# A hybrid encoder block on one core: new DRAM layouts in the mixer, attention scores over 128 partitions, and a different order of products, loads and stores

## The chip, the cores and the metric

The kernel runs on one core of one Trainium2 chip. The metric is the device time of one execution in microseconds (us); lower is better. All engines of the core work at once and meet through semaphores: TensorE (PE) multiplies, VectorE (DVE), ScalarE (ACT) and GpSimd (POOL) compute elementwise, and SyncE (SP) issues most of the transfers. ACT and POOL issue some as well.

## The reference

One layer for 1024 tokens of width 1024, all in float32:

```
h = h + 1/2 * SwiGLU(RMSNorm(h))
u = RMSNorm(h);  z = u @ W_in          # q | k | v | ssm input | gate_attn | gate_ssm
A = neighbourhood_attention(q, k, v)   # 8 heads of 64; 16 x 64 grid of tokens, window 8 x 16
B = s5_branch(ssm input)               # 32 groups of 16 channels, 64 complex states each,
                                       # forward and backward scan, + D*u, gelu, GLU (512 x 512)
h = h + (sig(gate_attn) * (A @ W_a) + sig(gate_ssm) * (B @ W_s)) @ W_out
h = h + 1/2 * SwiGLU(RMSNorm(h))
h = h + (p @ W_ple) * sig(RMSNorm(h) @ W_g);  out = RMSNorm(h)
```

## The kernel before, in words

Every large product is made of float32r matmuls. An operand is split into a high and a low part (ACT casts the high part, DVE subtracts for the low one), and three matmuls of 128x512 take high-high, high-low and low-high (`mm3`, L188; lines L190 to L192 in the profile). Large products are further folded into seven block products (Strassen-Winograd): of one pair of output blocks the seven run in the order of `A7`, into the PSUM accumulators `ACC7 = "ZXYXYXX"`. The sixth product (index 5) leaves the sum that becomes block 22 in X, DVE adds it out of X (`s_evac`, L1535), and the seventh product goes on accumulating in the same X.

The change lies in the **mixer**, the stage between the two feed-forward networks. The main code of the mixer emits these products on PE:

- `proj` (accumulator `sin`): 8 products of 24 matmuls, the input of the state-space branch. Their results go to the DRAM tile `u_d`.
- `value` (accumulator `v`): 8 products of 24 matmuls for v, each for 128 tokens; the results go to `v_d` as high and low part.
- `items`: 12 pairs times 7 block products of 12 matmuls (`px`, `py`, `pz`) for q, k and the gates; the weight blocks `blk` are loaded `LL` products ahead. Results go to `q_d`, `k_d` and `g_d`.

Beside it runs a generator, `mixer_side` (L1315). It holds everything else of the mixer, and the main code calls `tick()` after each step of three matmuls; a `yield n` in the generator lets n steps pass. So the numbers in the yields set how the side work is mixed into the in-order queue of PE: the norm of the second token half (`u_second`), the injections into the states (`inject`, 16 pairs of groups, accumulator `inj`), the attention (64 units of head, row half and column block: `attn_scores` into `s`, `attn_turn` into `pt` two units later, `attn_values` into `O` four units later), the recurrence on POOL (`scan_steps`), the read-out of the states (`ssm_out`, 16 pairs, accumulator `yo`), and the GLU (`glu_load`, `glu_half`, accumulator `glu`). Ahead of block product 78 of 84 stands `drain()`: whatever is left of the generator is emitted there in one piece, with no main product in between.

DVE, ACT, POOL and SP get their order from a scheduler at build time; PE keeps the order of the program. Each queue runs in order. A transfer that SP or ACT issues takes one of eight completion counters in turn (`DMAHW0` to `DMAHW7` in the rows further down) and waits for the last transfer on that counter.

## Time and profile before

| what | value |
|---|---|
| runs before | 2194.84 us median of 2 (2192.94 to 2196.74) |
| the profiled execution's own time | 2193.82 us |
| its span, first to last instruction | 2192.0 us |
| granted TensorE clock, mean over the span | 0.982 |
| PE busy | 2089.9 us, 95% of the span |
| DVE, ACT, POOL busy | 1465.8, 1015.1, 436.4 us |
| moved by transfers | 317.67 MB, 145 GB/s on average |

Times in the views are microseconds from the start of the span, durations of single instructions are nanoseconds where a view says so. A wait is idle time of an engine, put down to what ended it. Matmuls are pipelined: the time from one start to the next is what a matmul costs, not the duration of its row.

### The profile page before, as it was taken

Reading aid. Unit: us, or ns where it says so; the run is one execution under the profiler, and the core shown is the slowest. Engines: PE = TensorE matmul, PEld = TensorE weight load, DVE = VectorE, ACT = ScalarE, POOL = GpSimd, SP = SyncE. Lnnn points to the kernel's source line nnn. Section 1 sums busy time; section 2 is a strip of 40 time slices with the busy share of each in tenths; the row PEclk is TensorE's granted clock in tenths of the full one; section 3 lists DMA queues with packets and bytes.
Section 4 is the critical chain, followed back from the end, with each engine's and each line's share of the span. In section 5 each row is a group of like instructions: output and inputs, shape, how many; then the busy total and the mean of one; then the engine's idle time right before and its main releaser. Section 6 shows DMA issues by size and latency. Waiting matters only on the chain.

```text
span 2192.0 us, 28396 instructions
## 1 busy us (share of the span) xinstructions
PE 2089.9 (95%) x9518; PEld 1684.9 (77%) x9518; DVE 1465.8 (67%) x2470; ACT 1015.1 (46%) x1870; POOL 436.4 (20%) x652
## 2 busy tenths in 40 slices
PE   8999999999999798999993799999999999999998
PEld 3788888888887686777772588878888888888887
DVE  7897866767867545665550467897656655795855
ACT  6443333344454334666553464554333333545543
POOL 0046555530001328886000002000000000000000
PEclk9999999999999899999997899999999999999999
DMA  3434444496334475666555685324232337443302
GB/s 127 149 113 155 129 129 135 133 311 189 107 115 129 121 191 176 188 183 181 162 158 181 211 266 150 81 91 154 82 124 88 115 97 278 137 142 96 116 29 77
DMA packets 239859, 317.67 MB, mean 145 GB/s; under 512 B 55264, under 2 KB 113248, under 8 KB 239712
## 3 DMA queue, kind: packets, MB, share of 16 engines
q1 hardware_dynamic: 200592, 277.02, 40.6%
q10 hardware_dynamic: 36816, 34.63, 4.8%
q0 software_dynamic: 2304, 4.20, 1.1%
q8 instruction: 75, 1.23, 0.2%
q14 instruction: 72, 0.59, 0.1%
HBM read 221.92 MB, written 93.85 MB: 144 GB/s over the span
## 4 chain that ended last, share of the span: by engine, by line
PE 85%; DVE 6%; DMA 3%; SPq 2%; ACT 2%; issue 1%; POOL 0%; ACTq 0%; DVEq 0%
PE dx L190 4%; PE dx L191 4%; PE dx L192 4%; PE gx L190 3%; PE ux L190 3%; PE gx L192 3%; PE ux L192 3%; PE ux L191 3%; PE gx L191 3%; PE dy L191 2%; PE dy L192 2%; PE dy L190 2%; PE px L190 2%; PE px L191 2%; PE px L192 2%; PE gy L190 2%
## 5 line engine op out<-in xcount | busy, mean ns | idle before, releaser
L159 ACT CAST wh<-hbuf 128x512 fp32r<-128x512 f32 x280 | 173.0, 622 | 392.4 <-PE gx L191 84.1
L160 DVE TENSOR_TENSOR wl<-hbuf,wh 128x512 fp32r<-128x512 f32 x280 | 209.9, 752 | 123.6 <-ACT wh L159 121.2
L159 ACT CAST wh<-wblk 128x512 fp32r<-128x512 f32 x190 | 118.0, 622 | 191.2 <-PE dx L191 82.5
L190 PE MATMUL dx<-ah,wh 128*128 128x512 f32 x416 | 163.5, 393 | 0.4 <-DVE hbuf L694 0.3
L160 DVE TENSOR_TENSOR wl<-wblk,wh 128x512 fp32r<-128x512 f32 x190 | 130.5, 689 | 49.0 <-ACT wh L159 41.4
L192 PE MATMUL dx<-ah,wl 128*128 128x512 f32 x416 | 161.9, 389 | 0.0
L191 PE MATMUL dx<-al,wh 128*128 128x512 f32 x416 | 161.9, 389 | 0.0
L160 DVE TENSOR_TENSOR al<-araw,ah 128x512 fp32r<-128x512 f32 x154 | 106.1, 693 | 51.8 <-PE dx L191 21.2
L190 PE MATMUL gx<-xh,wh 128*128 128x512 f32 x320 | 124.9, 390 | 1.2 <-DVE c L581 1.2
L190 PE MATMUL ux<-xh,wh 128*128 128x512 f32 x320 | 125.0, 391 | 0.0
L192 PE MATMUL gx<-xh,wl 128*128 128x512 f32 x320 | 124.5, 389 | 0.0
L192 PE MATMUL ux<-xh,wl 128*128 128x512 f32 x320 | 124.5, 389 | 0.0
L191 PE MATMUL ux<-xl,wh 128*128 128x512 f32 x320 | 124.5, 389 | 0.0
L191 PE MATMUL gx<-xl,wh 128*128 128x512 f32 x320 | 124.5, 389 | 0.0
L159 ACT CAST ah<-araw 128x512 fp32r<-128x512 f32 x154 | 94.9, 619 | 47.1 <-PE dx L191 14.2
L1155 POOL TENSOR_TENSOR sc<-X,rho 128x128 f32<-128x128 f32 x128 | 77.7, 607 | 82.0 <-ACT X L1138 72.0
L190 PEld LDWEIGHTS dx<-ah,wh 128*128 128x128 f32 x416 | 78.1, 188 | 18.6 <-DVE hbuf L694 1.2
L428 DVE TENSOR_TENSOR hbuf<-hbuf 128x512 f32<-128x512 f32 x120 | 90.4, 754 | 2.7 <-DMA hbuf<-in_wu 0.6
L191 PEld LDWEIGHTS dx<-al,wh 128*128 128x128 f32 x416 | 78.1, 188 | 16.8 <-issue 0.7
L192 PEld LDWEIGHTS dx<-ah,wl 128*128 128x128 f32 x416 | 78.1, 188 | 16.3
L190 PE MATMUL px<-xh,wh 128*128 128x512 f32 x192 | 78.8, 410 | 12.1 <-DVE z L1535 11.2
L421 POOL DMA_DIRECT2D wblk<-in_wout x16 | 14.1, 934 | 339.5 <-ACT wblk L420 339.2
(396 smaller groups left out, 5785.7 us busy)
## 6 DMA issues: line engine op xcount, KB each, us to landing
araw<-a_d SPq DMA_DIRECT2D x154, 256.0 KB
a_d<-c SPq DMA_DIRECT2D x148, 256.0 KB
wblk<-in_wd SPq DMA_DIRECT2D x88, 256.0 KB
hbuf<-in_wg SPq DMA_DIRECT2D x40, 512.0 KB
hbuf<-in_wu SPq DMA_DIRECT2D x40, 512.0 KB
blk<-in_win SPq DMA_DIRECT2D x48, 256.0 KB
hbuf<-in_xT SPq DMA_DIRECT2D x32, 256.0 KB
h_d<-hbuf ACTq DMA_DIRECT2D x32, 256.0 KB
```

The lines of the kernel that those rows point to most:

```text
L159: A.copy(hi, src)
L160: return eng.tensor_tensor(lo, src, hi.bitcast(F32), ALU.subtract)
L190: T.matmul(o, lhsT=wh, rhs=xh, start=first, stop=False, skip_group_check=more)
L191: T.matmul(o, lhsT=wh, rhs=xl, start=False, stop=False, skip_group_check=more)
L192: T.matmul(o, lhsT=wl, rhs=xh, start=False, stop=last, skip_group_check=more)
L421: G.dma_start(blk[i], src, accum_op=ALU.add)
L428: V.tensor_tensor(b11, (b12, b22, None, None, b21)[i - 2], b11, ALU.subtract)
L1155: G.tensor_tensor(sc, both, rho4, ALU.mult)
```

## The change

All of it is in the mixer.

1. **Layouts in DRAM.** `u_d` and `y_d` become [4, 128, 8, 128] (channel, phase, chunk) and `v_d` becomes one block per head of 256 rows by 512. A store of `sin` and a load for the GLU are now one transfer of 128 partitions in place of eight of 16, and a load of v one transfer in place of four. The loads `ut` and the stores `ys` become two transfers of 64 KB in place of one of 128 KB.
2. **Scores.** One tile holds the high part of k in partitions 0 to 63 and the low part in 64 to 127; q is held as two tiles, the high part twice and the low part twice. Both matmuls of a score contract over 128 partitions. Before, the second one contracted over 64. The product of the two low parts is now included.
3. **Values.** Four accumulators are open at once and the weights go in the outer loop, so each weight block is loaded when it is near.
4. **Order of the block products.** The first product of a pair runs ahead of the last one of the pair before.
5. **Stores.** Stores of the gates, q and k are collected and issued at the third step of the next product; those of the gates all by SP.
6. **Mixing.** Injections take 2 steps each instead of 3, and all wait for the last `sin` store; an attention unit takes 3 steps instead of 4; the first loads of `ssm_out` go into the last units of the attention, and a pair of it takes 1 or 2 steps. The norm of the second half comes 4 steps earlier and its POOL part follows it, with the store of `s_d` issued by POOL.
7. **Buffers.** The pool `m` has 24 tiles (22), the pool `k4` two (3), and `LL` is 4 (5).

```diff
-    u_d = dtile("u_d", [NPD, P, NCH])
+    u_d = dtile("u_d", [4, P, L, NCH])
-    v_d = dtile("v_d", [SEQ, 1024])
+    v_d = dtile("v_d", [NH, 4 * GRID, 512])
-    y_d = dtile("y_d", [NPD, P, NCH])
+    y_d = dtile("y_d", [4, P, L, NCH])
...
     def u_second():
-        yield 10
+        yield 6
         un[1].stat()
         yield 1
+        for j in (0, 1, 2, 3, 4, 5, 6, 7):
+            u_norm(j, 1)
+            yield 1
+        yield 3
         for k in range(4):
-            u_norm(k, 1)
-            yield 1
-            u_norm(4 + k, 1)
             G.tensor_tensor(h[4 + k][1], h[k][1], h[4 + k][1], ALU.add)
...
     def load_u(pr):
         ut = ta("ut", [P, 2, NCH])
-        nc.sync.dma_start(ut, u_d[2 * pr:2 * pr + 2].rearrange("g p c -> p g c"))
+        for g in range(2):
+            i0 = (2 * pr + g) % 8 * 16
+            nc.sync.dma_start(ut[:, g], u_d[pr // 4, i0:i0 + 16].rearrange("i s c -> s i c"))
...
-            nc.scalar.dma_start(y_d[2 * pr:2 * pr + 2].rearrange("g p c -> p g c"), ys)
+            for g in range(2):
+                o0 = (2 * pr + g) % 8 * 16
+                nc.scalar.dma_start(y_d[pr // 4, o0:o0 + 16].rearrange("o t c -> t o c"), ys[:, g])
...
     def load_v(hd, cb):
-        for g in range(4):
-            nc.sync.dma_start(hl[0:n, g].bitcast(F32),
-                              vdr[4 * g:4 * g + 4, KC0[cb]:KC0[cb] + KNC[cb], hd * 128:(hd + 1) * 128])
+        nc.sync.dma_start(hl[0:n].rearrange("p g d -> p (g d)").bitcast(F32), vdr[hd, :, KC0[cb]:KC0[cb] + KNC[cb]])
...
-        T.matmul(s3, lhsT=q, rhs=kv(khs[hd]), start=True, stop=False)
-        T.matmul(s3, lhsT=q[ds], rhs=kv(kl_["t"])[ds], start=False, stop=True)
+        for a in range(2):
+            T.matmul(s3, lhsT=qs[hd, rb][a][:, ksl(cb)], rhs=kv, start=a == 0, stop=a == 1)
...
     def glu_load(t):
         for m in range(4):
             yt = ygs[t, m] = tmp("yt")
-            yv = yt.rearrange("p (t c) -> p t c", t=4)
-            for g in range(8):
-                nc.sync.dma_start(yv[g * 16:(g + 1) * 16], ydr[8 * m + g][:, 4 * t:4 * t + 4])
+            nc.sync.dma_start(yt, y_d[m, :, 4 * t:4 * t + 4].rearrange("p t c -> p (t c)"))
...
             inject(pr, *ld.pop(pr))
-            yield 3
+            yield 2
...
             scan_steps(2)
-            yield 4
+            if j >= n:
+                lo[j - n] = ssm_load(j - n) if j - n < 3 else None
+            yield 3
         scan_steps(NCH)
...
-            if 0 <= p - 1 < NPAIR:
+            if p > 0:
                 so.pop(p - 1)()
-            yield 2
+            yield 1 + p % 2
...
-            for g in range(8):
-                nc.sync.dma_start(u_d[8 * m + g].rearrange("(s i) c -> i s c", s=L)[:, :, t * 64:(t + 1) * 64],
-                                  su[g * 16:(g + 1) * 16].rearrange("i (s c) -> i s c", s=L))
+            nc.sync.dma_start(u_d[m, :, :, t * 64:(t + 1) * 64],
+                              su.rearrange("i (s c) -> i s c", s=L))
...
+    def values(t):
+        os_ = [bank("v") for _ in range(4)]
         for k in range(NK):
+            load_wv()
...
     items = [(n, i) for n in range(len(pairs)) for i in range(7)]
+    for n in range(7, len(items), 7):
+        items[n - 1:n + 1] = items[n], items[n - 1]
+    later = []
...
-            (nc.scalar if c == "21" else nc.sync).dma_start(g_d[2 * m + second, :, hsl(t)], src)
+            later.append((nc.sync, g_d[2 * m + second, :, hsl(t)], src))
...
             mm3(sacc[a], (hi[:, ksl(k)], lo[:, ksl(k)]), U[A7[i]][k], NEW7[i] and k == 0, k == 3, not NEW7[i])
+            if k == 2:
+                s_store()
+                if i == 1 and n > 0 and pairs[n - 1][0] == "qk":
+                    m = pairs[n - 1][1]
+                    ready.update((2 * m, 2 * m + 1))
             tick()
```

What that does to the queues is seen at three places. The first is PE at the end of a pair of blocks, here the gate pair `px_7784` before and `px_7782` after. Before, the seventh product (weights `wh_7943`) follows the sixth (`wh_7888`) at once:

```order
L190 MATMUL px_7784<-xh_7253,wh_7888 128x512
L191 MATMUL px_7784<-xl_7254,wh_7888 128x512
L192 MATMUL px_7784<-xh_7253,wl_7889 128x512
L190 MATMUL px_7784<-xh_7257,wh_7888 128x512
L191 MATMUL px_7784<-xl_7258,wh_7888 128x512
L192 MATMUL px_7784<-xh_7257,wl_7889 128x512
L190 MATMUL px_7784<-xh_6256,wh_7943 128x512
```

After the change the twelve matmuls of the next pair's first product (`pz_8132`) stand between; the seventh product of the pair (`wh_8036`) comes behind them:

```order
L190 MATMUL pz_8132<-xh_6007,wh_7977 128x512
L191 MATMUL pz_8132<-xl_6008,wh_7977 128x512
L192 MATMUL pz_8132<-xh_6007,wl_7978 128x512
L190 MATMUL px_7782<-xh_6251,wh_8036 128x512
L191 MATMUL px_7782<-xl_6252,wh_8036 128x512
L192 MATMUL px_7782<-xh_6251,wl_8037 128x512
```

So the seventh product has moved behind a product on another accumulator, at eleven of the twelve pairs.

The second place is PE at the first pairs of `ssm_out`. Before, the read-out follows the last main product ahead of the drain (`pz_11079`), pair behind pair:

```order
L190 MATMUL pz_11079<-xh_6007,wh_11017 128x512
L191 MATMUL pz_11079<-xl_6008,wh_11017 128x512
L192 MATMUL pz_11079<-xh_6007,wl_11018 128x512
L1181 MATMUL yo_11144<-ut_11114,emi_11110 128x128
L1183 MATMUL yo_11144<-xs_11128,emi_11110 128x128 x2
L1181 MATMUL yo_11144<-ut_11114,emi_11112 128x128
L1183 MATMUL yo_11144<-xs_11128,emi_11112 128x128 x2
L1181 MATMUL yo_11165<-ut_11120,emi_11116 128x128
L1183 MATMUL yo_11165<-xs_11139,emi_11116 128x128 x2
```

After the change main products (`px_10778`) stand between the pairs:

```order
L1182 MATMUL yo_10794<-ut_10649,emi_10645 128x128
L1184 MATMUL yo_10794<-xs_10752,emi_10645 128x128 x2
L1182 MATMUL yo_10794<-ut_10649,emi_10647 128x128
L1184 MATMUL yo_10794<-xs_10752,emi_10647 128x128 x2
L190 MATMUL px_10778<-xh_5782,wh_10706 128x512
L191 MATMUL px_10778<-xl_5783,wh_10706 128x512
L192 MATMUL px_10778<-xh_5782,wl_10707 128x512
L1182 MATMUL yo_10820<-ut_10679,emi_10675 128x128
L1184 MATMUL yo_10820<-xs_10789,emi_10675 128x128 x2
L1182 MATMUL yo_10820<-ut_10679,emi_10677 128x128
L1184 MATMUL yo_10820<-xs_10789,emi_10677 128x128 x2
```

What moved is the whole end of the generator: 39 main matmuls stand between the last `yo` and the first `glu`, six between each two of the eight GLU steps but the fourth and fifth, where 12 stand, and 87 behind the last GLU matmul, where 72 stood. The first score stands behind 141 main matmuls of the block products, before behind 123.

The third place is SP at the loads for the GLU (`yt`), here with the counters that each row waits for. Before, there are 64 of them, of which the first are:

```order
L1601 DMA hbuf<-h_d 128x512 [waits DMAHW4_49]
L1601 DMA hbuf<-h_d 128x512 [waits DMAHW5_49]
L1283 DMA yt<-y_d 16x4x128 [waits DMAHW7_49]
L1283 DMA yt<-y_d 16x4x128 [waits DMAHW0_49]
L1283 DMA yt<-y_d 16x4x128 [waits DMAHW1_49]
L1283 DMA yt<-y_d 16x4x128 [waits DMAHW2_49]
```

After the change there are eight, in two groups of four, behind seven loads of `hbuf` (the residual stream, 256 KB each):

```order
L1598 DMA hbuf<-h_d 128x512 [waits DMAHW2_49]
L1598 DMA hbuf<-h_d 128x512 [waits DMAHW3_49]
L1274 DMA yt<-y_d 128x512 [waits DMAHW4_49,PE_49]
L1274 DMA yt<-y_d 128x512 [waits DMAHW5_49,PE_49]
L1274 DMA yt<-y_d 128x512 [waits DMAHW6_49,PE_49]
L1274 DMA yt<-y_d 128x512 [waits DMAHW7_49,DMAHW1_49]
L1598 DMA hbuf<-h_d 128x512 [waits DMAHW0_49]
L1533 DMA g_d<-z_11240 128x512 [waits Activation_49]
```

Fifty-six issues are gone from SP there; the tiles that they filled are the same.

More of the change, by code (lines that the diff above doesn't have):

```diff
@@ L1316, in mixer_side @@
         yield from u_second()
[L1317 removed]
+        while 3 not in stored:
             yield 1
[L1319 removed]
+        yield 8
         new_x()
         ld = {}
+        for pr in range(2):
+            ld[pr] = inject_load(pr)
+        yield 6
         for pr in range(NPAIR):
[L1323 to L1330 removed]
+            if pr + 2 < NPAIR:
                 ld[pr + 2] = inject_load(pr + 2)
             inject(pr, *ld.pop(pr))
[L1333 removed]
+            yield 2
         while 0 not in ready:
@@ L1361, in mixer_side @@
                     load_k(hd + 1)
-                if rb == 1 and cb == 2 and hd + 1 < NH and hd + 1 not in khs:
+                if rb == 1 and cb == 2 and hd + 1 < NH and hd + 1 not in khl:
                     load_k(hd + 1)
@@ L1522, in s_out @@
         for i, x in enumerate((hi, lo)):
-            nc.scalar.dma_start((k_d if second else q_d)[m, i, :, hsl(t)], x.bitcast(F32))
+            later.append((nc.scalar, (k_d if second else q_d)[m, i, :, hsl(t)], x.bitcast(F32)))
     def s_evac(n, i):
@@ L1536, in s_evac, with s_store @@
         s_out(n, c, int(c[0]) - 1, int(c[1]) - 1, o[a] if c == "21" else z.pop(c))
+    def s_store():
+        while later:
+            q, dst, src = later.pop(0)
+            q.dma_start(dst, src)
     def s_run(n, i):
@@ L1547, in s_run @@
             s_evac(n, i)
-        if i == 6 and pairs[n][0] == "qk":
-            ready.update((2 * pairs[n][1], 2 * pairs[n][1] + 1))
-    LL, LP = 5, 2
+    LL, LP = 4, 2
     done_ = {"l": 0, "p": 0}
@@ L1560, in s_ahead @@
             done_["p"] += 1
-    for tt in range(NK):
-        if tt == 4:
-            s_ahead(-2)
-        if tt == 6:
-            s_ahead(0)
-        value(tt)
+    for t in range(2):
+        values(t)
     s3s = []
```

117 lines of the change are left out of this document (49 added, 68 removed).

## The prediction

> **What bounds the kernel now.** I read the busy shares first, then the mixer's stages by windows, then what PE waited for, then the rows at the places that the change touches. The page gives PE 95%, which says only that a loss must be looked for in single stages:
>
> ```profile
> PE 2089.9 (95%) x9518; PEld 1684.9 (77%) x9518; DVE 1465.8 (67%) x2470; ACT 1015.1 (46%) x1870; POOL 436.4 (20%) x652
> ```
>
> The mixer runs from 685.0 to 1265.9 us. Cut at the first matmuls of `sin`, `v`, the block products, the scores, `yo`, the idle stretch, `glu` and the last six block products:
>
> ```profile
> core 0: us, PE busy (x) PEld busy (x) DVE busy (x) ACT busy (x) POOL busy (x), PEclk, DMA share, GB/s
> 685.00:740.30 55.30, 48.68 (x203) 38.14 (x202) 44.03 (x47) 25.01 (x39) 26.98 (x16) 0.94 0.42 109
> 740.30:809.20 68.90, 61.08 (x314) 51.07 (x313) 23.06 (x46) 19.46 (x44) 4.13 (x11) 0.93 0.66 172
> 809.20:838.20 29.00, 28.12 (x124) 22.79 (x123) 21.89 (x29) 13.40 (x23) 25.63 (x44) 1.00 0.65 198
> 838.20:1139.50 301.30, 286.51 (x1518) 222.82 (x1518) 181.13 (x420) 176.56 (x389) 161.52 (x331) 0.99 0.59 174
> 1139.50:1176.30 36.80, 26.04 (x193) 23.93 (x191) 10.62 (x34) 19.49 (x49) 0.00 (x0) 0.95 0.84 254
> 1176.30:1209.90 33.60, 0.05 (x1) 0.00 (x0) 0.69 (x1) 7.81 (x12) 0.00 (x0) 0.56 0.35 105
> 1209.90:1244.70 34.80, 28.36 (x96) 21.40 (x97) 13.69 (x21) 13.85 (x23) 0.00 (x0) 0.84 0.56 180
> 1244.70:1265.90 21.20, 18.48 (x74) 14.50 (x72) 14.33 (x21) 11.86 (x19) 0.00 (x0) 0.92 1.03 275
> ```
>
> The sixth stage is the thing to see: 33.6 us without a matmul, every engine nearly idle. Around it the granted clock falls to 0.84 to 0.95. What PE waited for in the mixer:
>
> ```profile
> PE glu L190 <- ACT wgl L159: 39.5, 3, 33.6
> PE px L190 <- DVE z L1535: 11.2, 11, 2.4
> PE yo L1181 <- DMA ut<-u_d: 8.1, 9, 2.1
> PE py L190 <- ACT z L1531: 6.3, 2, 6.0
> PE sin L191 <- DVE xl L160: 5.0, 4, 2.6
> ```
>
> The releaser ACT `wgl` is only the last link: SP's timeline has 64 small issues of 0.48 us each, 30.44 us, and a weight load behind them.
>
> ```profile
> 1175.94 30.44 SPq L1283 DMA_DIRECT2D yt<-y_d  x64
> 833.38 12.38 SPq L1215 DMA_DIRECT2D vhl<-v_d  x16
> ```
>
> The second row is the same fault in the first loads of v. Block weights queue behind them, hence the one wait of 6.0 us above.
>
> **What the work itself costs.** One main matmul, from the first and the thirtieth in a row: (691.60 - 685.02) / 29 = 0.227 us.
>
> ```profile
> 685.02 0.39 PE L190 MATMUL sin<-xh,whh 128*128 128x512 f32 x1
> 691.60 0.39 PE L192 MATMUL sin<-xh,whl 128*128 128x512 f32 x1
> 771.08 1.05 PE L1131 MATMUL inj<-ut,fmi 128*128 128x128 f32 x8
> 771.89 0.48 PE L1439 MATMUL v<-wvh,xh 128*128 128x512 f32 x1
> 772.20 0.40 PE L1440 MATMUL v<-wvl,xh 128*128 128x512 f32 x1
> 1146.14 0.43 PE L1181 MATMUL yo<-ut,emi 128*128 128x128 f32 x2
> 1148.86 0.39 PE L1181 MATMUL yo<-ut,emi 128*128 128x128 f32 x2
> 1046.92 0.34 PE L1234 MATMUL s<-kh,qs 128*128 128x384 f32 x1
> 1047.19 0.44 PE L1235 MATMUL s<-kl,qs 64*128 64x384 f32 x1
> 1047.56 0.53 PE L1251 MATMUL pt<-ident,sm 128*96 128x128 f32 x3
> 1051.19 0.29 PE L1234 MATMUL s<-kh,qs 128*128 128x288 f32 x1
> ```
>
> An injection takes 0.81 us and slows the matmul behind it by 0.08, 0.89 together. Four half pairs of the read-out take 2.72 us, a pair 1.36. A unit of attention with 12 main matmuls takes 1051.19 - 1046.92 = 4.27; less 12 x 0.227, 1.55 are its own. So each stage has this much that is not work:
> - `sin`: 55.3 - 192 x 0.227 - 0.5 for the norm's sum = 11.2
> - `v`: 68.9 - 192 x 0.227 - 16 x 0.89 = 11.1
> - block products ahead of the scores: 29.0 - 123 x 0.227 = 1.1
> - attention: 301.3 - 813 x 0.227 - 64 x 1.55 = 17.5
> - `yo`: 36.8 - 16 x 1.36 = 15.0; the gap: 33.6; `glu`: 34.8 - 96 x 0.227 = 13.0; the last six: 21.2 - 72 x 0.227 = 4.9
>
> Together 107.4 us. PE's queue is in order and no main matmul is added or dropped; the change can take at most these 107 us and whatever a score gets cheaper.
>
> **The change part by part.**
>
> *GLU loads and the end of the generator.* 56 issues of 0.48 us, 27 us, leave SP. Next in line is a chain: store of the last `ys`, load `yt`, gelu, split. Rows of such links:
>
> ```profile
> 1176.79 3.04 DMA y_d<-ys
> 1206.43 2.83 DMA wgs<-in_wglu
> L1287 ACT ACTIVATE yt<-yt x8: 629/629/630, 1183.0 to 1208.0; 128x512 f32<-128x512 f32 x8
> ```
>
> Store 3.0, a load of 256 KB 2.8, one to four gelus 0.6 to 2.5, a split on ACT and DVE some 1.3: 7.7 to 9.6, plus seven loads of the residual on SP ahead of `yt` (at the 275 GB/s of the last window 1.8 MB are 6.7 us, part of which lies beside the store). So 9 to 16 us, against 39 main matmuls or 8.9 us. Left: 0 to 8, I take 3, nearest to the rows without a queue. The gap gives 30.6. In `glu` each step now has six main matmuls as cover and the clock stays up; the two other `wgl` waits are 39.5 - 33.6 = 5.9. Left 1 to 8, I take 4: gain 9.0. At the last six products 15 more matmuls stand between the GLU and its reader, so its splits are covered; left 2: gain 2.9.
>
> *Read-out.* 69 main matmuls stand between the pairs: PE needs 16 x 1.36 + 69 x 0.227 = 37.4 us, 2.34 a pair. The transfers:
>
> ```profile
> emi<-e_d SPq DMA_DIRECT2D x32, 192.0 KB
> ut<-u_d SPq DMA_DIRECT2D x32, 128.0 KB
> y_d<-ys ACTq DMA_DIRECT2D x16, 128.0 KB
> ```
>
> Two `emi`, one `ut` and one `ys` are 640 KB a pair as now; 0.36 main products add about 0.4 transfers, 105 KB. The window moved 254 GB/s at a share of 0.84, so 302 at a full one: 763 kB a pair need 2.53 us if all engines share them. Thirteen pairs (three are loaded in the attention's tail) at 0.2 over PE's need leave 2.5 us. Above, if `ut` and `ys` used half of the engines, their 262 kB count twice: 3.39 us a pair, 14 us left, 17 with the start. I take 8, since two facts lie between: 6.4 transfers a pair instead of 4 run on the same eight counters, and at a landing of 3.6 us (between the 2.46 and 4.66 below) they need 6.4 x 3.6 / 8 = 2.9 us. Gain 7.0.
>
> ```profile
> 1161.95 2.46 DMA ut<-u_d
> 1169.98 4.66 DMA ut<-u_d
> ```
>
> *Norm, `sin`, `v`, injections.* The sum of the norm starts 12 matmuls (2.7 us) earlier, the POOL work that ran beside DVE's norm comes after it, and four of the weight splits leave the first half. That removes the `xl` wait of 5.0 and the slow clock behind it; left 2 (0 to 5), gain 9.2. With `v`, a pair is injected every 2 x 0.68 + 0.89 = 2.25 us instead of 2.93, fed by 393 kB, 175 GB/s; in the second half the stores of the first four value blocks (2.1 MB in some 16 us, 133 GB/s) come on top. 308 is over the 172 / 0.66 = 261 GB/s of this window: 18% of 16 us is 3, and I leave 5 for this and the bank hand-over (2 to 10). Gain 6.1.
>
> *Attention.* The eleven `z` waits go behind a product of 2.7 us, and DVE's add is 0.7: hidden. What comes late next there is the copy of the first product, also behind a product. The v loads free SP: 4 issues instead of 16, and the 6.0 us go. With three steps a unit lasts 9 x 0.227 + 1.55 = 3.59 us. In it DVE has at most its present 181.13 / 64 = 2.8, ACT 2.8, POOL 2.5, less a quarter of the main part on the first two: none over 80%. The softmax between a score and its transpose two units later (7.2 us instead of 8.5) takes 0.5 + 0.6 + 0.2 + 0.6 = 1.9 plus queueing:
>
> ```profile
> L1239 DVE CUSTOM_DVE_ANT_0 sm<-s,tb x64: 435/500/558, 839.0 to 1121.7; 128x288 f32<-128x288 f32 x32, 128x384 f32<-128x384 f32 x32
> L1242 ACT ACTIVATE sm<-sm,stat x64: 532/576/622, 848.5 to 1122.6; 128x288 f32<-128x288 f32 x32, 128x384 f32<-128x384 f32 x32
> L1244 ACT ACTIVATE sm<-sm,stat x64: 523/568/620, 849.5 to 1123.7; 128x288 f32<-128x288 f32 x32, 128x384 f32<-128x384 f32 x32
> ```
>
> Left 6 (2 to 16), gain 11.5. The second score costs 0.37 to the next start, the first 0.27. Over 128 partitions it can cost the same 0.27 (64 x 0.10 = 6.4 gained) or still 0.37 (the step to transposes may be the reason, then 0); I take the middle, 3.
> The Trainium skill ("TensorEngine Tiling", Key Properties) says that a change of tiling mode drains TensorE. The 0.10 us agree with it; by it the whole 6.4 would go, and the sum would be 3 us lower.
>
> *Stores, pools.* Stores move behind the next product on SP and ACT, off PE's path; their cover is the same three steps. The smaller `k4` and `LL` cost nothing while blocks come two products ahead of their split.
>
> **Sum.** 9.2 + 6.1 + 0 + 11.5 + 3 + 7.0 + 30.6 + 9.0 + 2.9 = 79.3. From the profiled execution's 2193.8 (span 2192.0 and 1.8 around it; 1.0 under the median of the runs) that makes 2114.5 us, 3.6% faster. Two per cent, about what a measurement can tell from no change, is 44 us, the line at 2150.
>
> **Rivals.**
> - *Transfers pace injections and read-out.* 17 left instead of 8, 10 instead of 5, 8 instead of 3 ahead of the GLU: 19 more, 2133. For it speaks the share of 0.84 already now; against it, the three pairs loaded ahead. The Trainium skill ("DMA: Bandwidth & Descriptors", Why a DMA increments its semaphore by 16 and not by 1) lets a transfer run on as many engines, up to 16, as divide the outermost dimension of both patterns; the new `ut` and `ys` patterns begin with 8, so this rule is for it. No row here shows on how many engines a transfer ran.
> - *A unit doesn't get shorter.* If attention stays at 4.27 us through DVE, ACT, POOL or a late table, 64 x 0.68 = 43.5 are lost again: 2158, no change. Against it: busy shares under 0.6 in that window.
> - *The pair's wait only moves* to another accumulator: 8 us back, 2122, inside the forecast.
> - *Slower: stores on SP ahead of loads.* Already now SP stands before gate stores:
>
> ```profile
> SPq L1510 <- DVE z L1535: 54.7, 21, 8.2
> ```
>
> That is 2.6 us each on average. All 32 now go through SP, in front of tables, q, k, v and blocks that PE needs two units (7.2 us) later. If each store held SP for more than 7.2 + 79.3 / 32 = 9.7 us, all is lost and the kernel is slower; at 12, 32 x 4.8 = 154 come back, and the time is 2114.5 + 154 = 2268. Against it: a store is now emitted when its add is done, and 8.2 is the longest today.
> - *Nearly every wait hides:* 20 us more, 2095.
>
> **How the numbers follow.** Forecast 0.62, transfers 0.2, unit 0.08, hides 0.07, slower 0.03. The forecast's unknowns (0 to 8, 1 to 8, 2.5 to 17, 0 to 5, 2 to 10, 2 to 16, 0 to 6.4) don't all fall on one side; I take 2114 less 24 and plus 32, which holds the first, second and fourth case: 2090 to 2146. Faster by 2%: 0.62 + 0.2 + 0.07, and a sliver of the unit case off for long tails, 0.89; same 0.08; slower 0.03.
>
> **What would show it.** No stretch over 5 us without matmuls; no PE wait on L1535 but at the last pair; scores 3.6 us apart; `yo` pairs 2.3 to 2.9 apart; injections 2.3 apart; the first `glu` within 13 us of the last `yo`. I am wrong if PE now waits in many small pieces at `ut`, `s` or `pt`.

## The result, and the profile after

The changed kernel takes 2140.29 us (median of 2139.46 and 2141.12) against 2194.84 before: a ratio of 0.9751, with a 95% interval of 0.971 to 0.9793. The profiled execution took 2141.12 us with a span of 2139.2. The forecast was 2114, so the kernel got faster by 54.5 us where 79 were forecast; the range of 2090 to 2146 holds the time.

The page's first line, and the mixer cut at the same places as before (the stretch, its length, then busy time and instructions of PE, of PE's weight loads, of DVE, ACT and POOL, the granted clock, the share of the DMA engines, GB/s):

```profile
PE 2067.0 (97%) x9518; PEld 1687.7 (79%) x9518; DVE 1460.1 (68%) x2470; ACT 1011.7 (47%) x1870; POOL 436.4 (20%) x656
```

```profile
685.00:729.40 44.40, 44.40 (x195) 36.41 (x194) 37.13 (x37) 22.86 (x36) 28.91 (x20) 1.00 0.49 143
729.40:791.60 62.20, 59.16 (x322) 50.34 (x321) 26.63 (x55) 20.93 (x48) 8.08 (x19) 1.00 0.58 163
791.60:830.70 39.10, 34.44 (x142) 27.18 (x141) 24.11 (x33) 16.00 (x28) 34.16 (x64) 0.96 0.74 215
830.70:1081.00 250.30, 230.37 (x1330) 196.75 (x1330) 157.58 (x388) 160.45 (x366) 146.87 (x303) 0.95 0.65 195
1081.00:1131.00 50.00, 40.23 (x263) 34.46 (x262) 17.02 (x44) 22.51 (x54) 0.00 (x0) 1.00 0.69 206
1131.00:1150.90 19.90, 8.84 (x39) 6.95 (x37) 7.43 (x11) 11.19 (x19) 0.00 (x0) 0.85 0.98 334
1150.90:1188.00 37.10, 36.01 (x145) 28.31 (x146) 17.29 (x27) 15.29 (x25) 0.00 (x0) 0.94 0.48 160
1188.00:1213.00 25.00, 21.36 (x88) 17.20 (x87) 19.51 (x28) 16.82 (x27) 0.00 (x0) 0.94 0.98 256
```

The mixer lasts 528.0 us instead of 580.9; these 52.9 us are the whole gain. `sin` runs without a gap (44.40 busy of 44.40). The idle stretch of 33.6 us is now 19.9 us with 39 matmuls in it. In the attention PE is idle or slow for longer than before, though the stretch is shorter: 230 busy of 250 (20 idle, before 15), and a clock of 0.95 where it had 0.99. The records of the granted clock have it at one half four times there, 27 us in all, from 837.9, 885.6, 953.9 and 1025.6, each time at or just behind a wait of PE of 2.2 to 5.1 us. What PE waited for in the mixer:

```profile
PE pt L1245 <- ACT sm L1238: 12.8, 8, 4.5
PE glu L190 <- ACT wgl L159: 12.1, 3, 11.1
PE yo L1182 <- DMA ut<-u_d: 6.3, 5, 2.1
PE px L190 <- DVE z L1527: 3.6, 1, 3.6
PE inj L1132 <- DMA ut<-u_d: 3.0, 4, 1.1
```

The first line is new: the transposes of the attention wait for the softmax. The wait for a pair's last sum, eleven times before, is left once, at the last pair. How such a stall comes about is seen in one place of the timeline (start, duration, engine, line, operation, and in brackets the idle time before it with its releaser; SPq is SP issuing a transfer):

```profile
876.10 0.33 SPq L1490 DMA_DIRECT2D blk<-in_win  x1
...
882.79 0.34 PE L1229 MATMUL s<-khl,ql 128*128 128x384 f32 x1
...
886.25 0.69 DVE L430 TENSOR_TENSOR blk<-blk 128x512 f32<-128x512 f32 x1 [7.34 <-DMA blk<-in_win]
886.86 0.16 DVE L1237 RECIPROCAL stat<-stat 128x1 f32<-128x1 f32 x1
887.05 0.53 ACT L1238 ACTIVATE sm<-sm,stat 128x288 f32<-128x288 f32 x1 [7.21 <-DVE stat L1237]
...
887.63 0.66 PE L1245 MATMUL pt<-ident,sm 128*96 128x128 f32 x2 [4.50 <-ACT sm L1238]
```

A weight block issued at 876.10 lands at 886.15. DVE, in order, stands before it for 7.34 us; behind it in DVE's queue is the reciprocal of a softmax that has nothing to do with the block; ACT waits for the reciprocal and PE for ACT. The chain that ended last shows loads of blocks again and again between 827 and 1023 us, most of them for 6 to 12 us:

```profile
827.54 11.82 DMA blk<-in_win
876.10 10.05 DMA blk<-in_win
907.76 11.41 DMA blk<-in_win
...
937.85 11.23 DMA blk<-in_win
...
1000.72 8.51 DMA blk<-in_win
1016.22 6.24 DMA blk<-in_win
```

Before the change the chain had no load of a block between 800 and 1140 us. From the trace's records of issue and landing, between 840 and 1060 us, medians in us for one transfer (the longest block in brackets; the kernels of the last three lines are experiments). A v load is one transfer of 192 or 256 KB in the changed kernel and with blocks five ahead, and four transfers of a quarter of that in the other three:

| kernel | v transfers | weight blocks |
|---|---|---|
| before | 4.4 | 4.5 (7.0) |
| changed | 8.0 | 5.9 (11.4) |
| blocks five ahead | 8.1 | 6.2 (11.9) |
| v loads cut by columns | 4.3 | 4.3 (6.0) |
| v loads cut by rows | 2.5 | 3.9 (6.2) |

A whole v load, from its first issue to its last landing, takes 6.8 us before, 8.0 in the changed kernel, 6.7 cut by columns and 3.8 cut by rows (medians).

While stalls got longer, a unit of attention got shorter by more than the step it gave up. The first scores of two units that follow each other in the changed kernel:

```profile
879.35 0.34 PE L1229 MATMUL s<-khl,qh 128*128 128x384 f32 x1
879.53 0.34 PE L1229 MATMUL s<-khl,ql 128*128 128x384 f32 x1
879.71 0.49 PE L1245 MATMUL pt<-ident,sm 128*96 128x128 f32 x3
...
882.61 0.34 PE L1229 MATMUL s<-khl,qh 128*128 128x384 f32 x1
```

From score to score 0.18 us and from the second score to the transposes 0.18, where it was 0.27 and 0.37. Undisturbed units are 3.26 us apart behind a score of 384 columns and 3.19 behind one of 288, 3.22 on average, so 1.18 us are a unit's own beside nine main matmuls; before, 1.55 by the prediction's one unit of 384 columns.

### The profile page after: what moved, and what is told of

It is laid out like the page before. It is cut to its first block, busy times and chain, and to the rows that moved or that the text cites. A ratio compares the mean times of both kernels' runs of the same rounds, so it can differ in the third digit from the quotient of the medians.

```text
span 2139.2 us, 28212 instructions
## 1 busy us (share of the span) xinstructions
PE 2067.0 (97%) x9518; PEld 1687.7 (79%) x9518; DVE 1460.1 (68%) x2470; ACT 1011.7 (47%) x1870; POOL 436.4 (20%) x656
## 4 chain that ended last, share of the span: by engine, by line
PE 51%; DMA 7%; DVE 3%; ACT 2%; issue 1%; SPq 1%; ACTq 1%; DVEq 0%
DMA blk<-in_win 3%; PE dx L190 2%; PE dx L191 2%; PE dx L192 2%; PE ux L192 2%; PE gx L192 2%; PE gx L190 2%; PE ux L190 2%; PE ux L191 2%; PE gx L191 2%; PE br L190 1%; PE br L192 1%; PE br L191 1%; PE dy L191 1%; PE dy L192 1%; PE dy L190 1%
## 5 line engine op out<-in xcount | busy, mean ns | idle before, releaser
L160 DVE TENSOR_TENSOR wl<-wblk,wh 128x512 fp32r<-128x512 f32 x190 | 130.9, 692 | 50.2 <-ACT wh L159 42.5
L160 DVE TENSOR_TENSOR wl<-blk,wh 128x512 fp32r<-128x512 f32 x84 | 62.0, 739 | 80.8 <-ACT wh L159 76.6
L191 PEld LDWEIGHTS dx<-al,wh 128*128 128x128 f32 x416 | 78.1, 188 | 16.6 <-issue 0.7
L1156 POOL TENSOR_TENSOR sc<-X,rho 128x128 f32<-128x128 f32 x128 | 76.4, 597 | 62.7 <-ACT X L1139 52.8
```

Of the source, the lines that this page charges most:

```text
L160: return eng.tensor_tensor(lo, src, hi.bitcast(F32), ALU.subtract)
L191: T.matmul(o, lhsT=wh, rhs=xl, start=False, stop=False, skip_group_check=more)
L1156: G.tensor_tensor(sc, both, rho4, ALU.mult)
```

## The experiments

All times are medians; the ratio is to the kernel before, with its 95% interval. For each experiment the stretch that it acts on is shown too.

| kernel | us | ratio |
|---|---|---|
| `v_rows`: each v load in four transfers, by rows | 2115.00 | 0.9635 (0.9619 to 0.9651) |
| `five_ahead`: blocks loaded five products ahead | 2124.75 | 0.9678 (0.9663 to 0.9692) |
| `score_64`: second score over 64 partitions | 2141.48 | 0.976 (0.9739 to 0.9782) |
| `yield_4`: four steps a unit | 2150.42 | 0.9794 (0.978 to 0.9809) |
| `v_cols`: each v load in four transfers, by columns | 2140.23 | 0.9753 (0.9739 to 0.9766) |
| `v_rows_64`: v by rows, second score over 64 | 2133.75 | 0.9716 (0.97 to 0.9733) |
| `v_rows_five`: v by rows, blocks five ahead | 2118.64 | 0.9652 (0.9637 to 0.9666) |
| `v_rows_in_order`: v by rows, pairs not interleaved | 2118.21 | 0.965 (0.9635 to 0.9664) |
| `v_rows_y_old`: v by rows, old layout of `y_d` | 2128.15 | 0.9699 (0.9686 to 0.9713) |
| `v_rows_glu_w`: v by rows, GLU weights earlier | 2112.90 | 0.9627 (0.961 to 0.9645) |
| `best`: v by rows, GLU inputs and weights earlier | 2119.25 | 0.9655 (0.9641 to 0.9668) |
| `y_32`: v by rows, GLU weights earlier, old `y_d` read in 32 | 2107.24 | 0.9602 (0.9589 to 0.9615) |

**What makes the transfers late.** In the trace's records of counter steps a weight block has 16 steps as it lands. A load of v of the changed kernel has five: one 1 us after its issue and four when it lands. The records give times and not amounts; 16 in all, this reads as one step of 12 for engines that have no part in it and four of one, so the load is carried by four of the 16 DMA engines. Its pattern in DRAM begins with the 4 rows of a row group. That was so before as well, but then units were 4.2 us apart instead of 3.2.

The other transfers show what this does. The block of the timeline above, issued at 876.10, has twelve steps by 878.94 and its last four at 884.96, 885.42, 885.65 and 886.15. A v load issued at 874.81 has its four at 883.95, 884.41, 884.99 and 885.42. So twelve engines had carried their share of the block after 2.8 us, and four were 7 us later, when they were through with the v load. Between 840 and 1060 us the 26 blocks have their twelfth step at 3.3 us (median), the thirteenth at 5.4 and the last at 5.9; in `v_rows`, the experiment that follows, it is 3.1, 3.3 and 3.9, and tables, q and k are alike. Three v loads issued from 870.22 to 874.81 landed one behind the other, at 876.04, 880.13 and 885.42.

```diff
-        nc.sync.dma_start(hl[0:n].rearrange("p g d -> p (g d)").bitcast(F32), vdr[hd, :, KC0[cb]:KC0[cb] + KNC[cb]])
+        for r in range(4):
+            nc.sync.dma_start(hl[r * KNC[cb]:(r + 1) * KNC[cb]].rearrange("p g d -> p (g d)").bitcast(F32),
+                              vdr[hd, r, KC0[cb]:KC0[cb] + KNC[cb]])
```

> The changed kernel with one edit: each load of a head's values is four transfers of 24 or 32 rows (one for each of the four rows of the grid that a row group holds) in place of one transfer whose outermost dimension is 4. In the changed kernel these loads land 5.8 to 10.6 us after their issue in the stretches where they are issued, and the weight blocks, tables and queries queued with them 5 to 10 us. Theory A (the one wide transfer sits on 4 of the 16 DMA engines and holds up what follows on these; DVE and ACT, which take their work in order, then wait for a weight block ahead of a softmax, and TensorE waits for the softmax): the loads land within 5 us, the longest waits of DVE for a block fall from 7.3 us to under 3, the attention stretch of 250.1 us gets 15 to 25 us shorter, and the kernel comes to 2115 to 2126 us. Rival B (the weight blocks are asked for one product later than before, four ahead in place of five): the stretch stays within 5 us of 250 and the kernel at 2136 to 2144. Rival C (units 3.2 us apart leave the softmax too little time, whatever lands): as B. The four issues on SP instead of one cost nothing on TensorE under any of them, at most 2 us.

The kernel takes 2115.0 us, 25 less; a v transfer now has 16 counter steps (32 rows) or 13 (24 rows: one of 4 and 12 of one). The attention's row, and the transfers in the chain that ended last from 830 to 1057 us:

```profile
833.40:1057.50 224.10, 219.88 (x1329) 190.47 (x1328) 157.22 (x389) 159.01 (x365) 147.65 (x296) 0.99 0.72 214
```

```profile
892.83 2.69 DMA vhl<-v_d
896.50 5.98 DMA tb<-in_tabs
972.61 2.73 DMA vhl<-v_d
1053.56 2.57 DMA emi<-e_d
```

224 us instead of 250, the clock back at 0.99 (at one half for 3.4 us of the attention and not 27), no block left in the chain, DVE's longest wait for a block 2.3 us. Theory A's numbers came in, at the edge of its ranges or just over it (the stretch 26 us shorter, the longest load 5.5 us), 12 extra issues a head on SP and all. Is it the cut, or the number of engines?

```diff
-        nc.sync.dma_start(hl[0:n].rearrange("p g d -> p (g d)").bitcast(F32), vdr[hd, :, KC0[cb]:KC0[cb] + KNC[cb]])
+        for g in range(4):
+            nc.sync.dma_start(hl[0:n, g].bitcast(F32), vdr[hd, :, KC0[cb]:KC0[cb] + KNC[cb], g * 128:(g + 1) * 128])
```

> The changed kernel (2140 us) with each load of a head's values cut into four transfers by columns (512 bytes of every row each) in place of by rows: the outermost dimension of each transfer is 4 as in the one wide transfer, and there are four issues as in the cut by rows that gave 2115 us. Theory A (what counts is that the transfer runs on 4 DMA engines): nothing is gained, 2132 to 2146 us, since the same bytes go through the same engines; the attention stretch stays 245 to 255 us. Rival P (what counts is that one transfer of 256 KB is not cut, so that others can't come in between): as the cut by rows, 2112 to 2121 us, the stretch 222 to 230 us.

2140.2 us, as the changed kernel. Products ahead of the scores, attention, and the wait of the transposes:

```profile
790.80:838.60 47.80, 36.41 (x143) 28.47 (x142) 24.27 (x33) 15.86 (x28) 41.43 (x82) 0.89 0.69 199
838.60:1078.80 240.20, 225.04 (x1330) 192.57 (x1329) 154.33 (x387) 157.91 (x366) 140.67 (x286) 0.98 0.66 196
```

```profile
PE pt L1246 <- ACT sm L1239: 14.4, 13, 2.3
PE py L190 <- ACT z L1524: 8.5, 1, 8.5
```

The transposes wait oftener and shorter, and the attention alone is at 240, under what was expected. But the products ahead of it, where the first head's v is loaded, take 9 us more; both stretches together are 288.0 us, against 289.4 in the changed kernel and 267.0 in `v_rows`. A block now lands within 6 us of its issue. Still a whole v load takes 6.7 us (3.8 in `v_rows`), and DVE waits 11.0 us for blocks and 13.4 for tables in the attention (16.6 and 13.3 in the changed kernel, 5.2 and 4.4 in `v_rows`). So the cut alone is not what gains. Against `v_rows` this run differs in the engines and in the size of the pieces, 512 bytes in place of 2 KB. In the changed kernel the pieces are 2 KB as in `v_rows`, and there the steps of the blocks show the four engines late; what small pieces cost by themselves was not tried.

The Trainium skill ("DMA: Bandwidth & Descriptors", Why a DMA increments its semaphore by 16 and not by 1) gives this count, the largest number up to 16 that divides the outermost dimension of both patterns, and says that such a transfer takes the lowest-numbered engines. The counts of 4, 8, 12 and 16 in these traces agree with it. v loads that land one behind the other and four late steps in other transfers fit the same four engines each time; which engines they are, no record here shows.

**Was it the look-ahead?**

```diff
-    LL, LP = 4, 2
+    LL, LP = 5, 2
```

> The changed kernel with weight blocks loaded five products ahead, as before the change, in place of four; everything else as changed. Theory A (values' transfers on 4 DMA engines): a block that lands 10 us late instead of 4 is asked for 15 us earlier, so the waits of DVE for blocks fall, but tables, queries and values are late as before: the attention stretch gets 0 to 10 us shorter, 2130 to 2141 us in all. Rival B (the shorter look-ahead is the cause): the waits for blocks go and the stretch gets 15 to 25 us shorter, 2115 to 2126 us. Rival C (units too close together): no change, 2136 to 2144.

> The kernel with the values' loads in four transfers (2115 us), and in it weight blocks loaded five products ahead in place of four, which alone brought the changed kernel from 2140 to 2125 us. Theory A (the earlier load only made the blocks less sensitive to the values' transfers, so the two edits take away one and the same wait): 2110 to 2118 us. Rival B (a wait of its own, whose gain adds up): 2096 to 2104 us.

Alone it brings 15.5 us, more than theory A allowed and inside rival B's range. With the v loads cut by rows it brings nothing (2118.6 against 2115.0, intervals that overlap), which rules out a cost that adds to that of the v loads. The two edits take away the same wait: the blocks land as long after their issue as in the changed kernel (the table above), they are only asked for earlier. So the shorter look-ahead does have a part in it: with four ahead, late blocks cost 15.5 us that five ahead would have hidden. What DVE waits for in its attention has changed hands:

```profile
DVE sm L1233 <- DMA tb<-in_tabs: 19.8, 13, 4.0
```

In the changed kernel it was 16.6 us for blocks and 13.3 for tables.

**Are units too close together?**

```diff
-            yield 3
+            yield 4
```

> The changed kernel with four steps of three main matmuls between attention units in place of three. The attention then holds some 190 more main matmuls, and the stages behind it, which hold 339 between them, so many fewer. Theory A (values' transfers on 4 DMA engines): the same transfers are spread over a third more time, the stalls of 33 us in the attention fall to about 20, and what runs out of main matmuls behind it loses 5 to 20: 2130 to 2150 us. Rival C (units too close together for softmax and evacuation): the stalls fall to under 10 us, as before the change, and the kernel comes to 2115 to 2135 us. If the waits of the last stages are long because nothing is left to put beside them, 2150 to 2170 under either.

2150.4 us, where theory A's range ends and the case of the bare last stages begins. The wait of the transposes for the softmax falls from 12.8 to 2.7 us, but fewer main matmuls are left for the stages behind the attention, and the waits turn up there:

```profile
PE glu L190 <- ACT wgl L159: 19.8, 2, 16.4
PE yo L1182 <- DMA ut<-u_d: 14.8, 8, 4.7
```

By itself this does not tell A from C; `v_rows`, in which units stand as close as in the changed kernel (3.25 and 3.19 us) and the transposes wait 4.1 us in all, refutes C.

**What a score of 128 partitions is worth.**

```diff
-            T.matmul(s3, lhsT=qs[hd, rb][a][:, ksl(cb)], rhs=kv, start=a == 0, stop=a == 1)
+            k0 = P if a == 0 else 64
+            T.matmul(s3, lhsT=qs[hd, rb][a][0:k0, ksl(cb)], rhs=kv[0:k0], start=a == 0, stop=a == 1)
```

> The changed kernel with the second of a unit's two score products taken over 64 partitions only (the low half of the queries with the high half of the keys, as the kernel before computed it); the loads stay as they are, and the low half of the queries times the low half of the keys is left out. Theory M (going from 128 partitions to 64 and back costs TensorE the time by which the start-to-start times of the scores and of what follows them fell, from 0.269, 0.222, 0.373 and 0.325 us to 0.177, 0.133, 0.181 and 0.133): the distance of undisturbed units goes from 3.2 back to 3.6 us, and 64 units make 24 us: 2155 to 2166 us, or down to 2148 if a slower unit takes some of the stalls away. Rival N (the unit got shorter by something else, as by the order of its instructions or by what is resident beside them): the distance stays 3.2 us and the time 2136 to 2144.

> The kernel with the values' loads in four transfers (2115 us), and in it the second score product over 64 partitions again, leaving out the low half of the queries times the low half of the keys. With the wide loads of the changed kernel this edit cost 1 us, though its undisturbed units were 3.5 to 3.6 us apart in place of 3.2. Theory M + A (the mode change costs 0.37 us a unit, and in the changed kernel the late transfers set the attention's length, so that a shorter unit only waited more): with the transfers out of the way the attention stretch goes from 224 to 244 to 248 us and the time to 2135 to 2140 us. Rival T (transfers still set the attention's length): at most 8 us more, 2115 to 2123 us.

The scores of `score_64` are back at the old distances:

```profile
897.14 0.34 PE L1230 MATMUL s<-khl,qh 128*128 128x384 f32 x1
897.41 0.44 PE L1230 MATMUL s<-khl,ql 64*128 64x384 f32 x1
897.78 0.53 PE L1246 MATMUL pt<-ident,sm 128*96 128x128 f32 x3
...
900.73 0.34 PE L1230 MATMUL s<-khl,qh 128*128 128x384 f32 x1
```

3.59 us a unit instead of 3.26, 3.50 instead of 3.19, so 0.32 and 20 us over 64 units. Yet the kernel took 1 us more, not 15 to 26: the wait of the transposes fell from 12.8 to 2.9 us, the clock rose, and the attention lasted 251.7 us as before. With the v loads cut by rows the same edit costs 18.7 us, 17 of them in the attention (241.1 against 224.1), a little under what theory M with A expected (2135 to 2140) and far from rival T. So the step from 128 partitions to 64 and back has its price, and in the changed kernel it is paid out of stalls: late transfers set the attention's length there, and a shorter unit only waits longer.

**Interleaved pairs.**

```diff
-    for n in range(7, len(items), 7):
-        items[n - 1:n + 1] = items[n], items[n - 1]
```

> The kernel with the values' loads in four transfers (2115 us), and in it each pair's last product ahead of the next one's first again, as before the change. Theory S (TensorE's wait for the last sum of a pair, 11.2 us in eleven places before the change, is hidden by the product in between): it comes back, 1 us in each of eleven places, and the copy's wait at the front: 2124 to 2131 us. Rival H (with shorter units around it the waits fall where TensorE would wait anyway): 2112 to 2119 us.

```profile
PE px L190 <- DVE z L1527: 9.0, 8, 3.7
PE py L190 <- ACT z L1523: 2.2, 1, 2.2
```

The old waits return in eight places, 9.0 us. But with interleaving `v_rows` waits 3.7 us at the last pair and 4.7 for a copy of `z`; the difference of the waits is 2.8 us, and that of the times 3.2, too small to be told from nothing by these runs. The waits came back as theory S said; the time is in rival H's range and not in theory S's, because the interleaved order has waits of its own.

**The layout of `y_d`.**

```diff
-    y_d = dtile("y_d", [4, P, L, NCH])
+    y_d = dtile("y_d", [NPD, P, NCH])
...
-            for g in range(2):
-                o0 = (2 * pr + g) % 8 * 16
-                nc.scalar.dma_start(y_d[pr // 4, o0:o0 + 16].rearrange("o t c -> t o c"), ys[:, g])
+            nc.scalar.dma_start(y_d[2 * pr:2 * pr + 2].rearrange("g p c -> p g c"), ys)
...
-            nc.sync.dma_start(yt, y_d[m, :, 4 * t:4 * t + 4].rearrange("p t c -> p (t c)"))
+            yv = yt.rearrange("p (t c) -> p t c", t=4)
+            for g in range(8):
+                nc.sync.dma_start(yv[g * 16:(g + 1) * 16], ydr[8 * m + g][:, 4 * t:4 * t + 4])
```

> The kernel with the values' loads in four transfers by rows (2115 us), with the read-out's outputs laid out in DRAM as before the change: one store a pair, and 64 small loads for the GLU's inputs. Theory G (64 issues on SP of 0.48 us, 30.4 us before the change, hold back the GLU): the stretch from the last read-out to the first product of the GLU goes from 20 us to 38 to 48, the products inside it stay, and the time rises by 20 to 30 us to 2135 to 2145 us. Rival L (the issues are hidden by the 39 main matmuls and by the loads of the residual that now lie there): at most 8 us more, 2115 to 2123 us.

The read-out and the stretch up to the GLU:

```profile
1058.40:1099.10 40.70, 38.72 (x263) 34.34 (x262) 17.55 (x45) 22.61 (x55) 0.00 (x0) 1.00 0.83 253
1099.10:1140.80 41.70, 8.91 (x40) 7.03 (x38) 6.05 (x10) 10.94 (x18) 0.00 (x0) 0.66 0.48 153
```

As forecast the GLU comes 41.7 us after the read-out, instead of 19.6 in `v_rows`, 22 us later. But the read-out takes 40.7 us instead of 47.9, so the whole costs 13 us and not 20 to 30. With the new layout each store `ys` is two transfers of 64 KB whose counters have nine steps, read as one of 8 and eight of one: eight engines. One store of 128 KB with 16 steps takes the place of both in the old layout. The new layout is worth 22 us ahead of the GLU and costs 7 in the read-out.

**The stretch ahead of the GLU.** PE waits there for the split of the first weight, whose load SP issues only behind the loads of the inputs.

```diff
...
-            w = glu_w(k)
+            w = gw.pop(0) if gw else glu_w(k)
...
+        gw = [glu_w(0), glu_w(1)]
         yield 3
         glu_load(0)
```

> The kernel with the values' loads in four transfers (2115 us), and in it the first two weights of the GLU loaded and split right after the read-out's last pair is issued, ahead of the loads of its inputs, in place of behind them. TensorE waits 10.6 us for the first weight's split there. Theory W (the weight's load, queued on SP behind loads that wait for the read-out's stores, ends last): the GLU's first product starts when its first input has landed, gone through the gelu and been split, 4 to 7 us earlier: 2108 to 2111 us. Rival X (the window's transfers are the bound, at a share of 0.97, so that the inputs come later by what the weights come earlier): within 2 us, 2113 to 2117 us.

```profile
1104.00:1119.70 15.70, 8.96 (x41) 7.05 (x39) 7.11 (x11) 9.24 (x16) 0.00 (x0) 0.87 0.91 306
```

The first GLU product comes 15.7 us after the read-out instead of 19.6, a little less than theory W's 4 to 7 us earlier, and PE now waits 6.7 us for the inputs' split. The median fell by 2.1 us, inside the intervals: the place got shorter, the total is not shown to. Loading three inputs during the read-out as well goes too far:

```diff
+            if p in (6, 10, 14):
+                glu_in(0, p // 4 - 1)
+            if p in (8, 12, 16):
+                glu_act(0, [p // 4 - 2])
+            if p == 13:
+                gw = [glu_w(0), glu_w(1)]
...
```

> The kernel with the values' loads in four transfers by rows (2115 us), and in it three of the first four inputs of the GLU loaded during the read-out, each two pairs after its last pair was issued, their gelu two pairs later, and the first two GLU weights split during the read-out. Theory W (what TensorE waits for ahead of the GLU is a chain of loads behind the read-out's last store, though three quarters of the input were there before): the first GLU product starts 5 to 10 us after the last read-out in place of 20, the wait of 10.6 us goes, and 2101 to 2108 us come out. Rival X (the transfers of this window are the bound and the wait turns up at the read-out or later in the GLU): 2111 to 2117 us.

```profile
1104.90:1113.20 8.30, 2.86 (x14) 2.02 (x12) 2.91 (x6) 2.97 (x7) 0.00 (x0) 0.80 0.90 295
1113.20:1163.40 50.20, 40.10 (x144) 30.46 (x145) 18.37 (x28) 21.09 (x35) 0.00 (x0) 0.86 0.50 166
```

The GLU starts 8.3 us after the read-out and then takes 50.2 us instead of 37.3, waiting inside for weights (8.6 us) and splits (6.5): 2119.3 us, no faster than `v_rows` (the intervals overlap), and above both ranges. The wait moved, as rival X said.

**A version that takes the better half of both layouts** keeps one store a pair and reads it back in 32 transfers, half of them on POOL's queue, which is idle by then:

```diff
+            for i in range(4):
+                (nc.sync, nc.gpsimd)[i % 2].dma_start(yt[:, i * P:(i + 1) * P], ydr[8 * m:8 * m + 8, :, 4 * t + i])
...
```

> The kernel with the values' loads in four transfers by rows and the first GLU weights ahead of the GLU's inputs (2113 us), and in it the read-out's outputs again laid out as before the change, so that one store a pair runs on 16 DMA engines in place of two on 8, but read back by 32 transfers of 64 KB, half of them issued by SP and half by POOL, in place of 64 by SP. Theory Y (the old layout's read-out was 7 us shorter because its stores ran on 16 engines, and its GLU 22 us later because of 64 issues on SP): the read-out takes 40 to 42 us in place of 46, the first GLU product comes 14 to 20 us after it in place of 16, and the kernel comes to 2104 to 2112 us. Rival Z (the old layout's read-out was shorter only because the issues on SP came later and left the DMA engines to it): the read-out stays at 45 to 48 us, and the 32 issues make it 2113 to 2122 us.

```profile
1058.20:1099.60 41.40, 38.37 (x263) 34.43 (x262) 17.53 (x44) 22.57 (x54) 3.24 (x6) 1.00 0.84 255
1099.60:1118.80 19.20, 8.94 (x40) 7.05 (x38) 5.97 (x10) 8.99 (x16) 6.27 (x11) 0.86 0.85 257
```

41.4 and 19.2 us, both inside what theory Y expected: the stores made the read-out longer, not what SP issued in the meantime. Whether it was their eight engines or their number, two a pair in place of one, these runs do not tell apart. The traces speak for the number: a store of `ys` in the read-out lands after 3.8 us (median) in `v_rows`, 3.9 in `v_rows_y_old` and 4.1 here, so those on eight engines are not late. ACT's waits there that are put down to `ys` and `ut` transfers, whose counters its next store needs, are 15.0 us in `v_rows` and 2.2 in each of the other two. An estimate from these figures: 16 more transfers of 3.8 us on eight counters are 7.6 us. 2107.24 us, 0.9602 (0.9589 to 0.9615), is the fastest of all here, 33 us under the changed kernel.

## Why the prediction was right, and where it was not

Measured against the stages' work, as the prediction did it (main matmuls by 0.227 us and the side work's own time):

| stage | left, forecast | left, measured | gain, forecast | gain, measured |
|---|---|---|---|---|
| `sin` | 2 | 0.3 | 9.2 | 10.9 |
| `v` | 5 | 4.4 | 6.1 | 6.7 |
| products ahead of the scores | 1.1 | 7.1 | 0 | -6.0 |
| attention, stalls | 6 | 33.1 | 11.5 | -15.6 |
| attention, a unit's own work | | | 3 | 23.7 |
| `yo` | 8 | 12.6 | 7.0 | 2.4 |
| gap ahead of the GLU | 3 | 11.1 | 30.6 | 22.5 |
| `glu` | 4 | 4.4 | 9.0 | 8.6 |
| last six | 2 | 5.3 | 2.9 | -0.4 |
| sum | | | 79.3 | 52.8 |

The way and the rough size came out; 26.5 us of the gain did not. The gap holds 8 of them, the attention's two terms together 6, the products ahead of it 6, the read-out 5 and the last six 3; `sin` and `v` give 2 back.

- **`sin`, `v`, injections, `glu`: right.** Twelve of the fifteen steps from injection to injection are 2.27 us (2.25 forecast); the terms are within 2 us.
- **Attention, stalls: wrong, outside its bounds of 2 to 16.** The 33.1 us are about 20 of idle PE and half of the 27 at half the clock. The step that failed is "The v loads free SP: 4 issues instead of 16, and the 6.0 us go". It counted issues, but not how many DMA engines carry each. SP's time was freed and then lost to the landing: SP's waits in the attention that are put down to v loads sum to 29 us, against 5 before and 2 in `v_rows`. `v_cols` and `v_rows` both have the 16 issues back and are 25 us apart. Of the ahead-of-scores and attention stretches `v_rows` gives back 22 us (289.4 to 267.0).
- **The 6.0 us were misread too.** The prediction put them down to blocks that queue on SP. The chain before the change goes another way: a store of q on ACT waits for a v load to land (its counter is taken), ACT's queue stands 8.7 us before it, and the split of a weight and the copy of `z` come behind it.

```profile
839.13 5.46 DMA vhl<-v_d
844.67 0.33 ACTq L1523
847.24 0.79 PE py L190
```

In `v_rows` the same store holds ACT for 7.6 us, and PE waits 4.7:

```profile
828.75 0.62 ACT L159 CAST wh<-blk 128x512 fp32r<-128x512 f32 x1 [7.56 <-DMA vhl<-v_d]
```

In the changed kernel, with four v transfers there, ACT stands 4.1 us and PE 1.6, but the block issued at 827.54, behind the v loads, then costs PE 5.1 us at 840, in the attention.
- **Products ahead of the scores: 7.1 for 0.** This term had no loss in it. PE waits 3.0 us at 797: with four values open at once, ACT issues their eight stores in one go from 790.4 to 799.5 and casts the next weight only behind them. The 1.6 us above come later, and for 3.4 us behind the first wait the clock is at one half and main matmuls start 0.43 us apart in place of 0.23.
- **Look-ahead: wrong.** "The smaller `k4` and `LL` cost nothing while blocks come two products ahead of their split" put at nothing what `five_ahead` gives back in the changed kernel, 15.5 us. With v loads on time it costs nothing (`v_rows_five`).
- **A unit's own work: wrong, outside its bounds of 0 to 6.4, on the other side.** "Over 128 partitions it can cost the same 0.27" took 0.27 us for an undisturbed score. It was not: 384 columns at the main matmul's pace are 0.227 x 384/512 = 0.17 us, and 0.18 is what both now cost. Both starts around the 64-partition matmul were slow. `score_64` shows 20 us for the step to 64 partitions and back; the rest of the 23.7 is that 1.55 was read off a wide unit (1.50 over both widths).
- **The two errors, -27 and +21, nearly cancel.** They are not independent: with late transfers the attention lasts 250 to 252 us whether the unit is 3.2 us or 3.5 (`score_64`), so a shorter unit turns into stalls. But that the attention's sum came out within 7 us was luck, since neither error was foreseen. Over both edits the times are 2141.5 (64 partitions, wide loads), 2140.3 (128, wide), 2133.8 (64, by rows) and 2115.0 (128, by rows): either alone brings 1 or 8 us, both bring 26.
- **Read-out: the forecast's 8 became 12.6**, in its bounds of 2.5 to 17. The rival named the half-used engines, the forecast also the eight counters; `v_rows_y_old` and `y_32` put 5 to 7 us (40.7 for 47.9, 41.4 for 46.3) on the stores `ys` alone, and the landing times speak for the counters. What the two loads `ut` cost is open.
- **Gap: the forecast's 3 became 11.1**, over its bounds of 0 to 8. The chain ended with gelu and split; left out was the load of the GLU weight, which SP issues behind the inputs. `v_rows_glu_w` shortened the gap by 3.9 us, then the inputs are last. The chain of the changed kernel has the load:

```profile
1144.16 6.09 DMA wgs<-in_wglu
```

- **Last six: 5.3 for 2.** 3.6 of it is PE's wait for the last pair's sum (2.4 before): DVE's add stands behind splits of `br`, whose load takes 6.0 us in the chain.
- **Pairs interleaved:** the eleven waits went but for the last pair's, as forecast. That the new order has a wait of its own was left out; by `v_rows_in_order` the order is worth some 3 us, which is not clear of the noise.
- **Rivals.** "Transfers pace injections and read-out" (2133) was nearest to the time; its read-out and its gap lost what it said in kind (12.6 and 11.1 us, for 17 and 8), the injections did not, and the largest place, the attention, it did not name. "A unit doesn't get shorter" was refuted, 3.22 us apart. SP's longest wait before a gate store in the attention was 5.4 us, under the 9.7 from which the slower case would have decided.
- **What would show it:** injections and the waits on the last sum as forecast; two stretches of over 5 us without matmuls (11.1 and 5.1) and not none; scores 3.2 us apart and not 3.6; read-outs 2.0 to 4.3 and not 2.3 to 2.9; the GLU 20 us after the read-out and not 13. "I am wrong if PE now waits in many small pieces at `ut`, `s` or `pt`" named the place.

The Trainium skill ("TensorEngine Tiling", Key Properties) says that a change of tiling mode drains TensorE. The slow starts ahead of the 64-partition matmul and behind it agree with that. The prediction took 6.4 us for the whole price, from one of the two starts; the runs show some 20.

## What to carry to other kernels

Before fewer and wider transfers are counted as a gain, look at the outermost dimension of their patterns: one transfer of 256 KB that begins with a 4 was worse than four that begin with 24 or 32, and it was paid by another engine's softmax behind a late weight block in an in-order queue. The counter steps of the transfers beside it show such a place: most come early, and the same few late. Price a product by the pace of its neighbours (columns by the main matmul's time per column), not by its own row, which may hold a stall. An edit's worth depends on what binds: the same score edit was worth 1 us behind late transfers and 19 without them.

## What was not expected of the hardware

- Loads of 192 and 256 KB on four DMA engines landed in 8.0 us (median) and drew the median block from 3.9 to 5.9 us and the longest from 6.2 to 11.4, though the DMA engines' mean share was only 0.65.
- One 64-partition matmul between 128-partition ones cost 0.32 us a unit on top of its own time, nearly twice what the matmul takes (0.18): 0.09 at its own start (0.27 for 0.18), 0.19 at the start of the transposes behind it (0.37 for 0.18) and 0.04 in these (0.53 for three in place of 0.49).
- With stalls of 2 to 5 us the granted clock over the attention was 0.95, without them 0.99: a stall also slows what follows it. In the clock's records it is at one half for 3.4, 6.8 or 10.2 us at a time, from within a longer wait or just behind it; behind the wait of 3.0 us at 797 it was 3.4 us. Waits of 1.6 and 2.2 us (at 827 and 919) were followed by none.
